# The last layer's MLP: seven half products in three of four chunks, plain ones in the fourth, and low parts on VectorE

## The chip, the cores and the metric

The kernel runs on one core of a Trainium2 chip. The metric is device time in microseconds (us) of one execution. Five engines work side by side, each through its own instructions in order: TensorE (PE; its weight loads are shown as PEld), VectorE (DVE), ScalarE (ACT), GpSimd (POOL) and SyncE (SP), which here issues the DMA transfers. They wait for each other by semaphores. Before the change the median of three runs is 2346.34 us (2345.56 to 2347.01).

## The reference

Two layers of a transformer trunk with a token-mixing half (convolution branch and differential attention) and a channel half. The change touches only the channel half of the second layer, on 512 latent tokens:

```
def sqrelu_mlp(h, w1, w2):
    return jnp.square(jax.nn.relu(h @ w1)) @ w2
...
x = x + gx2 * sqrelu_mlp(modulate(rmsnorm(x, norm2_g[i]), sx2, ax2), w_mlp1[i], w_mlp2[i])
```

h has 1024 columns, w1 is 1024 x 4096 and w2 is 4096 x 1024. All of it is float32, and the result must be as exact as float32.

## The kernel before

**Three matmuls for one.** A float32 operand is split (`split`, lines 75 to 77) into a high part, which ScalarE writes in the format fp32r (L76), and a low part, the rest, which VectorE or GpSimd subtracts (L77). `mm3` then issues three matmuls into the same PSUM bank: high times high (L109), high times low of the moving operand (L110), low of the stationary operand times high (L111).

**Stages.** `last_mixing` takes the 4096 hidden columns in four chunks of 1024. In each chunk the *first products* (`hidden`) compute relu(h w1) squared in four slabs s of 256 columns, 48 matmuls of 512 columns a slab: 192 in a chunk. `operands` turns a slab's result fr into stationary operands. Then the *half products* multiply these with W2's chunk and add to what earlier chunks gave.

**Seven half products.** The chunk's second product is 512 tokens x 1024 by 1024 x 1024. It is cut into quarters: A11, A12, A21, A22 (halves of the tokens by halves of the hidden columns) and B11, B12, B21, B22 of W2. In place of eight products of quarters, seven are made (Winograd's form of Strassen's method): products 1 (A11 B11), 2 (A12 B21), 3 (S4 B22), 4 (A22 T4), 5 (S1 T1), 6 (S2 T2) and 7 (S3 T3), where S1 to S4 are sums of A's quarters (tile sm, L505 to L508) and T1 to T4 sums of B's (`minus`, L578, in place in the tiles r_w). One half product is 2 token tiles x 4 slabs x 3 = 24 matmuls. Products 2, 3 and 4 stay in their PSUM banks through all chunks (`held`); products 1, 5, 6 and 7 go to X, which is free by then (`summed`, L538). In the last chunk the seven are combined, multiplied with the gate row (grow), and x is added; x stands transposed in DRAM (xt_d) and is loaded back.

**Buffers and queues.** High and low parts of weights have two buffers each (tags whi, wlo), which W1's slabs and W2's quarters take in turn: ScalarE can start a new high part only when the last matmul that reads the buffer's former content is done. Raw weights have four buffers of 1 MB (tag raw). sm and aoh, aol (high and low parts of A11 and S1 to S4; A12 and A22 stand in h2hh and h2hl) have one. W2's quarters are split in two halves of 128 x 1024, the first half's low part on VectorE, the second's on GpSimd. The sums' low parts (aol<-sm) are on GpSimd too.

**Order.** A scheduler sets each engine's order when the program is built, from its own estimate of times; on the chip each engine then keeps to it. So an instruction that waits holds everything behind it on its engine.

In the trace, f is a first product, r a half product, h_ and l_ high and low parts (h_w: W1; h_b: a quarter as it is; h_t: a sum T).

## Time and profile before

| | |
|---|---|
| median of three runs | 2346.34 us |
| the profiled execution's own time | 2348.47 us |
| its span, first to last instruction's end | 2346.6 us |
| mean granted TensorE clock in the span | 0.99 |
| TensorE, VectorE, ScalarE, GpSimd busy | 96%, 68%, 44%, 35% |
| moved by DMA | 229.47 MB, mean 98 GB/s |

The span starts at 0; times in the views are us from there. The last layer's MLP begins at about 1974 us. A row of the timeline has the start, the duration, the engine, the line, the operation, the tiles written and read, and in brackets how long the engine had been idle and what ended that. A group row has count, busy us and mean ns of one, and the idle time before. Durations of instructions that follow each other at once overlap a little, so that the distance of their starts, not the duration, is what each costs. In a row of windows stand the stretch, its length, busy us and count of PE, PEld, DVE, ACT and POOL, the granted clock, the DMA engines' busy share and GB/s.

### The profile page before, as it was taken

Reading aid. Unit: us, or ns where it says so; the run is one execution under the profiler, and the core shown is the slowest. Engines: PE = TensorE matmul, PEld = TensorE weight load, DVE = VectorE, ACT = ScalarE, POOL = GpSimd, SP = SyncE. Lnnn points to the kernel's source line nnn. Section 1 sums busy time; section 2 is a strip of 40 time slices with the busy share of each in tenths; the row PEclk is TensorE's granted clock in tenths of the full one; section 3 lists DMA queues with packets and bytes.
Section 4 is the critical chain, followed back from the end, with each engine's and each line's share of the span. In section 5 each row is a group of like instructions: output and inputs, shape, how many; then the busy total and the mean of one; then the engine's idle time right before and its main releaser. Section 6 shows DMA issues by size and latency. Waiting matters only on the chain. (4 is left out here: it accounts for less than half of the span.)

```text
span 2346.6 us, 36460 instructions
## 1 busy us (share of the span) xinstructions
PE 2256.7 (96%) x14530; PEld 2019.1 (86%) x14530; DVE 1586.3 (68%) x2690; ACT 1036.2 (44%) x2007; POOL 813.6 (35%) x843
## 2 busy tenths in 40 slices
PE   8999999999999999999999999999999999999996
PEld 6999998888888998888888998899877779787785
DVE  6777776599666455655546567867769876646658
ACT  5555655522332362332415255656533334554442
POOL 1866764110000142323232266757510001423426
PEclk9999999999999999999999999999999999999999
DMA  9211111134535124333334311210115333233131
GB/s 303 63 36 44 46 46 45 46 128 154 178 125 185 43 80 135 108 126 117 117 117 135 91 62 43 59 44 26 61 54 165 112 115 128 90 126 108 57 128 67
DMA packets 216937, 229.47 MB, mean 98 GB/s; under 512 B 7408, under 2 KB 195776, under 8 KB 216640
## 3 DMA queue, kind: packets, MB, share of 16 engines
q1 hardware_dynamic: 216768, 227.15, 30.4%
q8 instruction: 114, 1.87, 0.3%
q14 instruction: 55, 0.45, 0.1%
HBM read 211.36 MB, written 15.77 MB: 97 GB/s over the span
## 5 line engine op out<-in xcount | busy, mean ns | idle before, releaser
L109 PE MATMUL f<-h2hh,h_w 128*128 128x512 f32 (+1 forms) x832 | 282.1, 342 | 1.7 <-ACT h2hh L76 1.5
L110 PE MATMUL f<-h2hl,h_w 128*128 128x512 f32 (+1 forms) x832 | 282.7, 341 | 1.0 <-POOL h2hl L77 1.0
L111 PE MATMUL f<-h2hh,l_w 128*128 128x512 f32 (+1 forms) x832 | 281.5, 340 | 0.0
L77 POOL TENSOR_TENSOR l_w<-r_w,h_w 128x1024 fp32r<-128x1024 f32 x64 | 157.5, 2482 | 336.5 <-ACT h_w L76 336.5
L1166 DVE SCALAR_TENSOR_TENSOR cacc<-z,cols,cacc 128x783 f32<-128x783 f32 (+1 forms) x240 | 207.9, 918 | 0.3
L109 PE MATMUL qk<-h_wqk,h1h 128*128 128x256 f32 x640 | 183.3, 289 | 2.1 <-ACT rw L758 1.4
L109 PE MATMUL r<-fh,h_w 128*128 128x256 f32 (+1 forms) x576 | 183.7, 319 | 0.3 <-DVE X L1363 0.3
L110 PE MATMUL r<-fl,h_w 128*128 128x256 f32 (+1 forms) x576 | 183.4, 319 | 0.0
L111 PE MATMUL r<-fh,l_w 128*128 128x256 f32 (+1 forms) x576 | 183.2, 318 | 0.0
L110 PE MATMUL qk<-l_wqk,h1h 128*128 128x256 f32 x640 | 180.7, 285 | 0.0
L111 PE MATMUL qk<-h_wqk,h1l 128*128 128x256 f32 x640 | 176.9, 285 | 0.3 <-POOL h1l L77 0.3
L109 PEld LDWEIGHTS f<-h2hh,h_w 128*128 128x128 f32 x832 | 156.6, 189 | 20.3 <-ACT h2hh L76 1.9
L110 PEld LDWEIGHTS f<-h2hl,h_w 128*128 128x128 f32 x832 | 157.5, 190 | 19.3 <-POOL h2hl L77 1.9
L930 DVE TENSOR_REDUCE st<-S 128x1 f32<-128x768 f32 (+1 forms) x160 | 134.4, 845 | 58.5 <-PE S L928 57.3
L111 PEld LDWEIGHTS f<-h2hh,l_w 128*128 128x128 f32 x832 | 157.3, 189 | 17.7
L282 DVE SCALAR_TENSOR_TENSOR adaac<-ar,cvec,adaac 128x256 f32<-128x256 f32 x336 | 152.1, 516 | 20.5 <-ACT adaac L279 15.0
L933 ACT ACTIVATE e<-S,st 128x768 f32<-128x768 f32 (+1 forms) x160 | 130.8, 820 | 39.9 <-DVE st L930 39.7
L76 ACT ACTIVATE h_w<-r_w 128x1024 fp32r<-128x1024 f32 x96 | 96.4, 1052 | 102.5 <-issue 55.2
L109 PE MATMUL gt<-h1h,h_wg 128*128 128x512 f32 (+1 forms) x384 | 138.0, 360 | 0.0
L110 PE MATMUL gt<-h1l,h_wg 128*128 128x512 f32 (+1 forms) x384 | 136.7, 356 | 0.0
L111 PE MATMUL gt<-h1h,l_wg 128*128 128x512 f32 (+1 forms) x384 | 136.6, 356 | 0.0
L109 PEld LDWEIGHTS qk<-h_wqk,h1h 128*128 128x128 f32 x640 | 122.8, 192 | 4.5 <-ACT rw L758 1.6
(316 smaller groups left out, 6795.8 us busy)
## 6 DMA issues: line engine op xcount, KB each, us to landing
r_w<-in_w_mlp_dram SPq DMA_DIRECT2D x64, 1024.0 KB, 5.3
ada<-in_w_ada_dram SPq DMA_DIRECT2D x24, 1024.0 KB, 5.5
ar<-in_w_ada_dram SPq DMA_DIRECT2D x48, 512.0 KB, 3.5
r_wqk<-in_w_in_dram SPq DMA_DIRECT2D x32, 512.0 KB, 5.2
r_wg<-in_w_in_dram SPq DMA_DIRECT2D x16, 1024.0 KB, 5.2
r_wv<-in_w_in_dram SPq DMA_DIRECT2D x8, 1024.0 KB, 5.3
r_wao<-in_w_attn_out_dram SPq DMA_DIRECT2D x8, 1024.0 KB, 5.1
r_wo<-in_w_out_dram SPq DMA_DIRECT2D x8, 1024.0 KB, 5.2
```

Of the source, the lines that this page charges most:

```text
L76: nc.scalar.activation(out=hi, in_=src, func=AF.Copy)
L77: return (lo_eng or nc.vector).tensor_tensor(out=lo, in0=src, in1=f32(hi), op=ALU.subtract)
L109: nc.tensor.matmul(ps, sh, mh, start=first, stop=False)
L110: nc.tensor.matmul(ps, sh, ml, start=False, stop=False)
L111: nc.tensor.matmul(ps, sl, mh, start=False, stop=last)
L282: nc.vector.scalar_tensor_tensor(out=a[:, q], in0=r[:, j], scalar=cvec[:, k, q : q + 1], in1=a[:, q], op0=ALU.mult, op1=ALU.add)
L930: nc.vector.tensor_reduce(out=st[:, m : m + 1], in_=S[:, :nkey], axis=AX.X, op=ALU.max, negate=True)
L933: nc.scalar.activation(out=e[:, :nkey], in_=S[:, :nkey], func=AF.Exp, bias=st[:, m : m + 1], accum_out=st[:, 2 + m : 3 + m])
L1166: nc.vector.scalar_tensor_tensor(out=ca[cc][:, :CV], in0=zt[cc][:, t : t + CV], scalar=wcol, in1=ca[cc][:, :CV], op0=ALU.mult, op1=ALU.add)
```

## The change

In chunks 0 to 2 the seven half products stay. All low parts of W2's quarters and of the sums are now on VectorE, and B11 is loaded and split beside the last slab's first products. In chunk 3, the eight plain products are made: A's quarters are split straight from fr, no sums of A or B are built. The sums of the seven products of chunks 0 to 2 are combined at the head of chunk 3 (`combine`), beside its first products: they are gated, and x is added. The held banks of products 2, 3 and 4 take three quarters' plain products on top of what they hold, C22 gets a bank of its own. Each finished 128 x 512 tile then needs a multiplication with the gate row, an addition and two transfers (`final`). The core of the diff:

```
         def operands(c, s):
...
+            if c == 3:
+                split(AB[0][:, :2, s], AB[1][:, :2, s],
+                      fr[:, 0].rearrange("p (o n) -> p o n", o=2))
+                split(AT[0][:, :, s], AT[1][:, :, s],
+                      fr[:, 1].rearrange("p (o n) -> p o n", o=2))
+                return
...
-            split(AB[0][:, 1:, s], AB[1][:, 1:, s], sm, nc.gpsimd)
+            split(AB[0][:, 1:, s], AB[1][:, 1:, s], sm)
...
-            for k, eng in ((slice(0, 2), nc.vector), (slice(2, 4), nc.gpsimd)):
-                split(hi[:, k], lo[:, k], r[:, k], eng)
+            for k in (slice(0, 2), slice(2, 4)):
+                split(hi[:, k], lo[:, k], r[:, k])
...
+        def combine(step):
+            qs = ((0, 0), (0, 1)) if step == 0 else ((1, 0), (1, 1))
+            xq = fp.tile([P, 2, 2, HN], F32, tag="raw", bufs=4, name=f"xq{step}")
+            nc.sync.dma_start(xq, xt_d[2 * step : 2 * step + 2].rearrange("t h p n -> p t h n"))
+            for t in range(2):
+                m1, m5, m6, m7 = (M[n][:, t] for n in (1, 5, 6, 7))
+                if step == 0:
+                    tt(out=m6, in0=m1, in1=m6, op=ALU.add)
+                    tt(out=m7, in0=m6, in1=m7, op=ALU.add)
+                    tt(out=m6, in0=m6, in1=m5, op=ALU.add)
+                    tt(out=m5, in0=m7, in1=m5, op=ALU.add)
+                for (tq, nq), m in zip(qs, (m1, m6) if step == 0 else (m7, m5)):
+                    tt(out=m, in0=m, in1=gn[nq], op=ALU.mult)
+                    tt(out=m, in0=m, in1=xq[:, t, nq], op=ALU.add)
...
                         for m in range(2):
                             hidden(c, s, m, g)
+                            if (s, m) == (3, 0):
+                                b11 = quarter(c, 0, 0)
+                                w11 = halves_of(b11, f"b11_{c}")
...
+                if c == 3 and ss[0] < 2:
+                    combine(ss[0])
...
+        def final(tq, nq, t):
+            row = (2 * tq + t) * P
+            for j, o in enumerate((slice(0, 256), slice(256, 512))):
+                u = state["xp"].tile([P, 512], F32, tag="u", bufs=3,
+                                     name=f"u{tq}{nq}{t}_{j}")[:, :256]
+                tt(out=u, in0=banks[tq, nq][t][:, o], in1=gn[nq][:, o], op=ALU.mult)
+                tt(out=u, in0=u, in1=parts[tq, nq][:, t, o], op=ALU.add)
+                nc.sync.dma_start(
+                    out[0, row : row + P, HN * nq + o.start : HN * nq + o.stop], u)
+
+        for nq in range(2):
+            for kh in range(2):
+                w = w11 if (kh, nq) == (0, 0) else halves_of(quarter(3, kh, nq), f"b{kh}{nq}_3")
+                for tq in range(2):
+                    a = ((A11, A12), (A21, A22))[tq][kh]
+                    for t in range(2):
+                        product(banks[tq, nq][t], a, w, t, (tq, nq, kh) == (1, 1, 0), kh == 1)
+                        if kh:
+                            final(tq, nq, t)
```

Removed are the last chunk's seven products with the combining that stood between and behind them (before: L600 to L644). Every instruction ahead of the last layer's MLP stands where it did. Three places in the new order follow. In them the first number behind a tile's name is the chunk or the product, the last one only a running number.

VectorE in chunk 1, from the last rows of the first products' operands on (r_w2_1_00 and r_w2_1_11 are the raw tiles of B11 and B22, r1_1_0 is product 1's first tile). Before:

```order
L77 TENSOR_TENSOR aol_20749<-fr1_3_21683,aoh_20748 128x256
L578 TENSOR_TENSOR r_w2_1_01_21751<-r_w2_1_11_21753,r_w2_1_01_21751 128x1024
L506 TENSOR_TENSOR sm1_3_21738<-fr1_3_21683 128x256
L77 TENSOR_TENSOR l_b22_1_21794<-r_w2_1_11_21753,h_b22_1_21793 128x1024
L578 TENSOR_TENSOR r_w2_1_11_21753<-r_w2_1_11_21753,r_w2_1_00_21749 128x1024
L538 TENSOR_TENSOR X2_20130<-X2_20130,r1_1_0_21763 128x512
L505 TENSOR_TENSOR sm1_3_21738<-fr1_3_21683 128x256
```

Now:

```order
L514 TENSOR_TENSOR sm1_2_21664<-fr1_2_21609,sm1_2_21664 128x256
L77 TENSOR_TENSOR aol_20749<-sm1_2_21664,aoh_20748 128x4x256
L77 TENSOR_TENSOR l_b22_1_21794<-r_w2_1_11_21759,h_b22_1_21793 128x1024
L512 TENSOR_TENSOR sm1_3_21746<-fr1_3_21683 128x256
L77 TENSOR_TENSOR l_b22_1_21794<-r_w2_1_11_21759,h_b22_1_21793 128x1024
L543 TENSOR_TENSOR X2_20130<-X2_20130,r1_1_0_21763 128x512
L597 TENSOR_TENSOR r_w2_1_11_21759<-r_w2_1_11_21759,r_w2_1_00_21711 128x1024
L511 TENSOR_TENSOR sm1_3_21746<-fr1_3_21683 128x256
L77 TENSOR_TENSOR h2hl1_20141<-fr1_3_21683,h2hh1_20140 128x2x256
L597 TENSOR_TENSOR r_w2_1_11_21759<-r_w2_1_11_21759,r_w2_1_00_21711 128x1024
L543 TENSOR_TENSOR X2_20130<-X2_20130,r1_1_1_21777 128x512
L513 TENSOR_TENSOR sm1_3_21746<-sm1_3_21746,fr1_3_21683 128x256
```

The low part of sm2 and both halves of B22's low part are now VectorE's, and they stand ahead of the sum T2 (L597, before L578). Behind the last row come T1's low part (two halves), sm3's last row (L514) and sm3's low part.

TensorE in chunk 1, where the held product 3 ends and product 2 (B21) begins. Before:

```order
L109 MATMUL r1_5_1_21845<-h_t1_1_21825,aoh_20748 128x512
L111 MATMUL r_3_0_21255<-h_b22_1_21793,aol_20749 128x512
L111 MATMUL r_3_1_21268<-h_b22_1_21793,aol_20749 128x512
L110 MATMUL r1_5_0_21831<-l_t1_1_21826,aoh_20748 128x512
L111 MATMUL r1_5_0_21831<-h_t1_1_21825,aol_20749 128x512
L109 MATMUL r1_5_0_21831<-h_t1_1_21825,aoh_20748 128x512
```

Now:

```order
L111 MATMUL r_3_0_21255<-h_b22_1_21793,aol_20749 128x512
L111 MATMUL r_3_1_21268<-h_b22_1_21793,aol_20749 128x512
L111 MATMUL r1_5_0_21831<-h_t1_1_21825,aol_20749 128x512
L111 MATMUL r1_5_1_21845<-h_t1_1_21825,aol_20749 128x512
L109 MATMUL r_2_0_21325<-h_b21_1_21861,h2hh1_20140 128x512
L109 MATMUL r_2_1_21338<-h_b21_1_21861,h2hh1_20140 128x512
L110 MATMUL r_2_0_21325<-l_b21_1_21862,h2hh1_20140 128x512
```

Before, twelve matmuls of product 5 stood between product 3's last L111 and product 2's first L109. Now nearly all of product 5 is ahead of them, and two stand between.

VectorE at the end of the program (r_4 are product 4's banks, r3_1 the new bank of C22's second tile; u are the output tiles). Before:

```order
L605 TENSOR_TENSOR X2_20130<-X2_20130,grow_20750 128x512
L635 TENSOR_TENSOR X2_20130<-X2_20130,r_2_1_21338 128x512
L643 TENSOR_TENSOR u0_0_23100<-u0_0_23100,X2_20130 128x256
L643 TENSOR_TENSOR u0_1_23104<-u0_1_23104,X2_20130 128x256
L606 TENSOR_TENSOR X2_20130<-X2_20130,x2_22985 128x512
L605 TENSOR_TENSOR X2_20130<-X2_20130,grow_20750 128x512
L643 TENSOR_TENSOR u1_0_23120<-u1_0_23120,X2_20130 128x256
L606 TENSOR_TENSOR X2_20130<-X2_20130,x11_22877 128x512
L642 TENSOR_TENSOR u1_1_23124<-r_4_1_21406,grow_20750 128x256
L643 TENSOR_TENSOR u1_1_23124<-u1_1_23124,X2_20130 128x256
```

Now:

```order
L628 TENSOR_TENSOR u110_0_23087<-r3_0_22833,grow_20750 128x256
L628 TENSOR_TENSOR u110_1_23091<-r3_0_22833,grow_20750 128x256
L629 TENSOR_TENSOR u110_0_23087<-u110_0_23087,X2_20130 128x256
L629 TENSOR_TENSOR u110_1_23091<-u110_1_23091,X2_20130 128x256
L628 TENSOR_TENSOR u111_0_23107<-r3_1_22834,grow_20750 128x256
L628 TENSOR_TENSOR u111_1_23111<-r3_1_22834,grow_20750 128x256
L629 TENSOR_TENSOR u111_0_23107<-u111_0_23107,X2_20130 128x256
L629 TENSOR_TENSOR u111_1_23111<-u111_1_23111,X2_20130 128x256
```

The rows of 512 columns that combined products have moved ahead, into chunk 3's first products. Behind the last half product's tile stand only its four rows of 256 columns.

## The prediction

> **What bounds the kernel now.** I read the page first, then the stages of the last layer's MLP in the view of windows, then the timeline around the places where TensorE stands still.

> ```profile
> span 2346.6 us, 36460 instructions
> PE 2256.7 (96%) x14530; PEld 2019.1 (86%) x14530; DVE 1586.3 (68%) x2690; ACT 1036.2 (44%) x2007; POOL 813.6 (35%) x843
> ...
> core 0: us, PE busy (x) PEld busy (x) DVE busy (x) ACT busy (x) POOL busy (x), PEclk, DMA share, GB/s
> 2026.04:2069.06 43.02, 40.12 (x169) 32.29 (x168) 21.64 (x18) 20.46 (x25) 20.53 (x8) 0.96 0.33 100
> 2069.06:2112.58 43.52, 43.52 (x193) 36.04 (x192) 24.02 (x30) 23.35 (x34) 7.42 (x4) 1.00 0.29 96
> 2112.58:2155.94 43.36, 39.29 (x170) 31.17 (x168) 29.27 (x25) 16.85 (x18) 21.35 (x8) 1.00 0.33 99
> 2199.46:2243.23 43.77, 40.33 (x169) 32.38 (x168) 27.51 (x25) 16.84 (x18) 20.23 (x8) 0.96 0.31 97
> 2243.23:2286.75 43.52, 43.52 (x193) 36.05 (x193) 24.71 (x31) 22.87 (x33) 7.42 (x4) 1.00 0.29 97
> 2286.75:2332.22 45.47, 39.77 (x169) 30.91 (x167) 38.13 (x35) 14.84 (x16) 32.73 (x14) 1.00 0.18 58
> 2332.22:2346.60 14.38, 0.00 (x1) 0.00 (x0) 11.54 (x18) 0.00 (x0) 7.40 (x5) 0.61 0.31 109
> ```

> TensorE bounds the whole span (96%), so only its idle time, its matmul count and the end after its last matmul can pay. The 43.52 us rows are first products (192 matmuls, one more straddles): no idle, 43.52/192 = 0.2267 us a matmul. The rows of 43.02, 43.36 and 43.77 us are the seven half products of chunks 0, 1 and 2: 168 x 0.2267 = 38.1 us of matmul, so 4.9, 5.3 and 5.7 us lost. Chunk 3 takes 45.47 us for the same 38.1 (7.4 lost), and then come 14.38 us without TensorE. In all 37.7 us here are not matmul. Why they are lost, in chunk 1:

> ```profile
> 2112.13 0.39 PE L110 MATMUL f<-h2hl,h_w 128*128 128x512 f32 x1
> ...
> 2112.40 2.57 POOL L77 TENSOR_TENSOR aol<-sm,aoh 128x1024 fp32r<-128x1024 f32 x1 [6.14 <-ACT aoh L76]
> 2112.56 2.01 ACT L76 ACTIVATE h_b<-r_w 128x1024 fp32r<-128x1024 f32 x2 [0.23 <-PE f L110]
> ...
> 2114.92 2.37 POOL L77 TENSOR_TENSOR l_b<-r_w,h_b 128x1024 fp32r<-128x1024 f32 x1
> 2115.00 2.57 DVE L506 TENSOR_TENSOR sm<-fr 128x256 f32<-128x256 f32 x1 [2.31 <-POOL aol L77]
> ...
> 2115.30 0.61 PE L109 MATMUL r<-h_b,aoh 128*128 128x512 f32 x2
> ...
> 2117.50 1.21 DVE L77 TENSOR_TENSOR l_b<-r_w,h_b 128x1024 fp32r<-128x1024 f32 x1
> ...
> 2118.77 0.50 PE L110 MATMUL r<-l_b,aoh 128*128 128x512 f32 x1 [2.85 <-DVE l_b L77]
> ...
> 2126.17 0.61 PE L109 MATMUL r<-h_t,aoh 128*128 128x512 f32 x2
> 2127.07 0.73 PE L111 MATMUL r<-h_b,aol 128*128 128x512 f32 x2 [0.29 <-POOL aol L77]
> 2128.16 0.50 PE L110 MATMUL r<-l_t,aoh 128*128 128x512 f32 x1 [0.35 <-DVE l_t L77]
> ```

> TensorE waits 2.85 us for the low part of B22 from VectorE. VectorE could have made it at 2113.6, when ACT's first h_b was done, but stood behind L506, which waits for GpSimd's aol (one sm buffer), and then L506 itself took 2.57 us while GpSimd ran l_b. At 2127 and 2128 the next low parts are late in the same way. So the root is GpSimd: its own slow low parts, and VectorE slowed beside it:

> ```profile
> 2102.77 1.23 DVE L77 TENSOR_TENSOR l_b<-r_w,h_b 128x1024 fp32r<-128x1024 f32 x1 [2.61 <-ACT h_b L76]
> 2104.03 3.32 DVE L578 TENSOR_TENSOR r_w<-r_w,r_w 128x1024 f32<-128x1024 f32 x1
> ...
> 2107.61 1.21 DVE L578 TENSOR_TENSOR r_w<-r_w,r_w 128x1024 f32<-128x1024 f32 x1
> 2108.74 0.68 DVE L77 TENSOR_TENSOR h2hl<-fr,h2hh 128x512 fp32r<-128x512 f32 x1
> 2109.35 0.41 DVE L507 TENSOR_TENSOR sm<-sm,fr 128x256 f32<-128x256 f32 x1
> 2109.68 1.21 DVE L578 TENSOR_TENSOR r_w<-r_w,r_w 128x1024 f32<-128x1024 f32 x1
> ...
> L578 DVE TENSOR_TENSOR r_w<-r_w,r_w 128x1024 f32<-128x1024 f32 x32 | 55.1, 1723 | 0.4
> ...
> L77 POOL TENSOR_TENSOR aol<-sm,aoh 128x1024 fp32r<-128x1024 f32 x16 | 39.1, 2442 | 163.5 <-ACT aoh L76 156.2 <-PE r L111 7.3
> ```

> The same L578 takes 1.21 us alone and 3.32 us when a GpSimd low part runs; its mean is 1.72. Read by starts, VectorE alone needs 1.13 us for a 1024-wide row, 0.61 for 512, 0.33 for 256.

> **Chunks 0 to 2, worked out.** Seven second halves and four sums' low parts a chunk go from GpSimd (2.44 us or more each) to VectorE: 11 x 1.13 = 12.4 us. VectorE is busy 24.0 + 29.3 of chunk 1's 86.9 us, and loses the slow-downs, so it has room; only order matters. [...] I call the end of the first products 0 and walk chunk 1 in the changed order.

> VectorE before that: B11's low part starts at 2102.77, which is -9.8. From there eleven instructions (six of 1.13, one of 0.61, four of 0.33) end near -1.0 with sm2. ACT makes its high part (1.06), VectorE its low one: to 1.3. ACT's B22 halves follow at 1.2 and 2.2. Then VectorE: B22 low first half to 2.5, sm3 row, second half to 4.0, the sum of product 1 (0.61), a B row, two short ones, a B row: 7.9, product 1's other sum 8.5, sm row 8.8, T1's low first half about 10.0, its second 11.1, sm3's last row 11.5, ACT 12.6, low part 13.8.

> TensorE: product 1's first tile to 2.7, two L109 of product 3 (high part there at 1.2), the second tile to 5.9, product 3 to 9.5 with low parts there at 2.5 and 4.0: **the 2.85 us wait is gone**. Two L109 of product 5 to 10.0, then L110 needs T1's low part at 10.0 to 10.1: 0.15 us at most. Product 3's last L111 is the 70th matmul: 69 x 0.2267 + 0.15 = 15.8; sm3's low part is there at 13.8.

> A **new wait** comes at B21. Its high tile takes B22's buffer (two buffers), so ACT can start only after product 3's last L111. Above, ACT follows the last reader's start by 2112.56 - 2112.13 = 0.43 us, and takes 1.0: 15.8 + 1.45 = 17.3. TensorE's order has only two matmuls of product 5 between, and is there at 72 x 0.2267 + 0.15 = 16.5: waits 0.8. Two L109 later it needs the low part (17.3 + 1.25 = 18.5; TensorE at 17.75): another 0.8. Before, 12 matmuls of product 5 stood ahead of that L109 and 10 more ahead of the low part, and hid both. After it nothing waits: T3's low part comes at 22, needed at 24. A restart costs about 0.1 once. So 38.1 + 0.15 + 0.8 + 0.8 + 0.1 = 40.0 us; chunk 2 has the same order; in chunk 0 ACT copies the sums, and T1 comes earlier (39.9). Three times 40.0 against 130.15 us: **-10.1**. No wait over 1 us is left, so I also count no time at a lower clock: the clock column has 0.96 only in stages with such a wait (chunks 0 and 2; chunks 1 and 3 have it and 1.00). Bounds: 0 us of waits (-15.9), and all as now (0).

> **Chunk 3.** One half product more: 24 x 0.2267 = +5.4. Against it all 7.4 us of its stalls, if nothing new waits. The operands are plain splits without sm. B11 is split while the last first products run; 42 matmuls of it remain (9.5 us) and cover the next quarter (ACT 2.0 + VectorE 1.1 after the buffer is released, 3.6 us). Each later quarter has 48 matmuls (10.9 us) of cover. So 192 x 0.2267 = 43.5 against 45.47: **-2.0**. The 24 combining rows (24 x 0.61 = 14.6 us) move into the first products' stretch, where VectorE is idle 43.52 - 24.71 = 18.8 us, and loses the sm rows there. Their two x transfers go ahead of W1's second and third slab on SP, each about

> ```profile
> r_w<-in_w_mlp_dram SPq DMA_DIRECT2D x64, 1024.0 KB, 5.3
> ```

> long; the slab behind xq0's buffer starts when the combining lets it go, about 19 us in, and is needed at 8 x 24 x 0.2267 x 3/4 = 32.6: 24.3 plus 2 for the halves fits by 6 us. I take 0; bounds 0 and 3.

> **The end.**

> ```profile
> 2331.83 0.40 PE L111 MATMUL r<-h_t,h2hl 128*128 128x512 f32 x1
> ...
> 2333.43 0.68 DVE L605 TENSOR_TENSOR X<-X,grow 128x512 f32<-128x512 f32 x1
> ...
> 2337.37 1.07 DVE L642 TENSOR_TENSOR u<-r,grow 128x256 f32<-128x256 f32 x3
> ...
> 2343.37 0.42 DVE L643 TENSOR_TENSOR u<-u,X 128x256 f32<-128x256 f32 x1
> 2343.82 0.33 SPq L644 DMA_DIRECT2D out_dram<-u  x1
> ...
> out_dram<-u SPq DMA_DIRECT2D x4, 128.0 KB, 1.7
> ```

> VectorE works off combining for 11.5 us after the last matmul. Changed, only four 256-wide rows follow it: 0.1 + 3 x 0.33 + 0.42 = 1.5, issue at once, 1.7 to landing, and 1.1 from that landing (2345.5) to the span's end: 4.3, with 0.2 for the matmul end and a u buffer (three, a 1.7 us transfer each): 4.5. **-9.9**; bounds 3.9 and 7.5 (if the last row waits a whole transfer).

> Sum -10.1 - 2.0 - 9.9 = **-22.0**: span 2324.6. The profiled execution took 2348.47 us by its own clock, 2.1 over the median of 2346.34, so I take the difference from the median: **2324.3 us**.

> **Rivals.** (1) *The move buys nothing in chunks 0 to 2*: VectorE's queue takes over what GpSimd did, and TensorE waits 5.3 us a chunk as now. For: the new wait at B21, and a one-engine queue. Against: L506's wait and the 3.32 us rows vanish with GpSimd. 2334.4 us, 0.10.
> (2) *No wait is left in them*: if the buffers are released sooner or VectorE runs ahead, 3 x 1.9 = 5.7 less: 2318.6, 0.10.
> (3) *Slower: VectorE becomes the bound*. If L578's 1.72 us mean is its own and not GpSimd's doing, VectorE stays that slow and the added halves and low parts ahead of B21 (B22, T1, B21, sm2, sm3) stand on the path: 5 x 1.72 = 8.6 us more wait a chunk, 25.8 - 11.9 = +13.9: 2360 us. It turns slower from 11.9/3 = 4.0 us a chunk. Against: two rows of 1.21 us in the same stage with GpSimd idle. 0.03.
> (4) *The last chunk starves*: xq or a W1 slab late, or the final rows held by three u buffers; 5 to 10 us: about 2332, 0.10.
> The rest, 0.67, is my forecast with its own range of 2320 to 2329.

> **Numbers.** No change within 0.2% means 2341.6 to 2351.0; it needs (1) and (4) together and more: 0.04. Slower 0.03, faster 0.93. The range that takes in the bounds of the waits and most of (1) and (4): 2318 to 2333.

> **What would show it.** Right: the product stages of chunks 0 to 2 near 40 us with a wait of about 0.8 us at h_b and one at l_b of B21, none of 2.85; clock 1.00 in them; no GpSimd row after norm 2; L597 at 1.2 us; 192 gapless matmuls in chunk 3; 4 to 5 us from the last matmul to the end. Wrong: a wait at l_t of product 5 over 1 us (VectorE late), a gap before a first product of chunk 3 (x or W1 late), L597 near 1.7, a tail over 7.

## The result, and the profile after

The changed kernel takes **2327.78 us** (median of six runs, 2325.58 to 2331.33), and the kernel before 2347.19 us in the runs beside it: ratio **0.9917, interval 0.9904 to 0.9929**, that is 19.4 us less. Predicted were 2324.3 us, with 2318 to 2333 as the range. The profiled execution took 2328.47 us with a span of 2326.7 us, 19.9 less than before's 2346.6.

The page of the changed kernel begins:

```profile
span 2326.7 us, 36416 instructions
...
PE 2256.1 (97%) x14554; PEld 2021.1 (87%) x14554; DVE 1572.8 (68%) x2720; ACT 1026.7 (44%) x1997; POOL 682.5 (29%) x789
```

The same view of windows as in the prediction, cut at the start of each stage's first matmul. Rows: product stage of chunk 0, first products of chunk 1, product stage of chunk 1, product stage of chunk 2, chunk 3's first products (with six early matmuls of B11 among them), the rest of chunk 3's products, the end.

```profile
core 0: us, PE busy (x) PEld busy (x) DVE busy (x) ACT busy (x) POOL busy (x), PEclk, DMA share, GB/s
2026.08:2065.94 39.86, 38.64 (x170) 31.38 (x169) 25.28 (x25) 20.39 (x26) 0.00 (x0) 1.00 0.35 109
2065.94:2109.46 43.52, 43.52 (x194) 36.04 (x193) 24.14 (x33) 23.20 (x33) 0.00 (x0) 1.00 0.29 94
2109.46:2149.74 40.28, 38.73 (x170) 31.30 (x169) 29.65 (x32) 16.78 (x19) 0.00 (x0) 1.00 0.35 107
2193.26:2235.19 41.93, 40.37 (x170) 32.46 (x168) 30.32 (x33) 16.77 (x19) 0.00 (x0) 0.96 0.32 103
2235.19:2280.07 44.88, 44.88 (x200) 37.16 (x198) 28.41 (x40) 20.77 (x30) 0.00 (x0) 1.00 0.41 138
2280.07:2322.40 42.33, 42.32 (x187) 34.72 (x185) 17.84 (x35) 7.75 (x9) 0.00 (x0) 1.00 0.13 43
2322.40:2326.70 4.30, 0.00 (x0) 0.00 (x0) 1.42 (x4) 0.00 (x0) 0.00 (x0) 0.88 0.22 73
```

GpSimd has no row left in any of them. Where the time went, by stage:

| Stage | before | changed | difference | predicted |
|---|---|---|---|---|
| products of chunk 0 | 43.02 | 39.86 | -3.16 | -3.0 |
| products of chunk 1 | 43.36 | 40.28 | -3.08 | -3.4 |
| products of chunk 2 | 43.77 | 41.93 | **-1.84** | -3.8 |
| chunk 3, first products and products | 43.52 + 45.47 | 44.88 + 42.33 | -1.78 | -2.0 |
| the end | 14.38 | 4.30 | -10.08 | -9.9 |
| sum | | | -19.9 | -22.0 |

The products began at 2026.04 us before and at 2026.08 after, so nothing came from ahead of them. One row is off: chunk 2, and its clock column says 0.96 where chunks 0 and 1 say 1.00.

What TensorE waited for between 2026 and 2322 us, in the view of waits (total, times, longest):

```profile
PE r L110 <- DVE l_b L77: 2.2, 3, 0.9
PE r L109 <- ACT h_b L76: 2.1, 3, 0.7
```

Once a chunk each: these are the two waits at B21. The 2.85 us wait for B22's low part is gone, and nothing else of this size is left. The timeline of chunk 2 at that place:

```profile
2209.20 0.61 PE L111 MATMUL r<-h_t,aol 128*128 128x512 f32 x2
2209.40 2.01 ACT L76 ACTIVATE h_b<-r_w 128x1024 fp32r<-128x1024 f32 x2 [3.71 <-PE r L111]
2209.63 1.29 DVE L543 TENSOR_TENSOR X<-X,r 128x512 f32<-128x512 f32 x2 [2.68 <-PE r L111]
2210.51 0.73 PE L109 MATMUL r<-h_b,h2hh 128*128 128x512 f32 x2 [0.69 <-ACT h_b L76]
2210.83 2.35 DVE L77 TENSOR_TENSOR l_b<-r_w,h_b 128x1024 fp32r<-128x1024 f32 x2
...
2212.11 0.50 PE L110 MATMUL r<-l_b,h2hh 128*128 128x512 f32 x1 [0.86 <-DVE l_b L77]
...
2213.24 0.63 PE L111 MATMUL r<-h_b,h2hl 128*128 128x512 f32 x1
2213.66 0.63 PE L109 MATMUL r<-h_b,h2hh 128*128 128x512 f32 x1
2214.09 0.63 PE L110 MATMUL r<-l_b,h2hh 128*128 128x512 f32 x1
```

ACT can begin B21's high part only when product 3's last L111 has let go of the buffer (2209.40), and TensorE has two matmuls of product 5 to do meanwhile. By starts of matmuls (0.23 us apart where nothing waits) it loses 0.85 us there. VectorE then still has two L543 rows, the sums of product 5, ahead of the low part: 1.03 us more. After 2213 the matmuls stand 0.42 us apart in place of 0.23, though nothing is late any more: TensorE runs at half its clock (0.50 in the clock column from 2213.01 to 2216.43 us, quoted below). In chunk 1 the same two waits (0.85 and 1.03 us) were followed by matmuls 0.23 us apart.

VectorE alone, two groups between 1973 and 2327 us:

```profile
L597 DVE TENSOR_TENSOR r_w<-r_w,r_w 128x1024 f32<-128x1024 f32 x24 | 29.1, 1218 | 0.0
L512 DVE TENSOR_TENSOR sm<-fr 128x256 f32<-128x256 f32 x12 | 5.1, 422 | 6.5 <-ACT fr L497 6.1
```

The sum over W2 (before: L578 with a mean of 1723 ns) takes 1218 ns, L512 422 (before: L506 with 955), and neither waits for GpSimd. The end:

```profile
2322.00 0.39 PE L111 MATMUL r<-h_b,h2hl 128*128 128x512 f32 x1
2322.43 0.76 DVE L628 TENSOR_TENSOR u<-r,grow 128x256 f32<-128x256 f32 x2 [1.30 <-PE r L111]
2323.10 0.75 DVE L629 TENSOR_TENSOR u<-u,X 128x256 f32<-128x256 f32 x2
2323.54 0.81 SPq L630 DMA_DIRECT2D out_dram<-u  x2
```

Four short rows follow the last matmul, as the order says.

### The profile page after: what moved, and what is told of

It is laid out like the page before. It is cut to its first block, busy times and chain, and to the rows that moved or that the text cites. A ratio compares the mean times of both kernels' runs of the same rounds, so it can differ in the third digit from the quotient of the medians.

```text
span 2326.7 us, 36416 instructions
## 1 busy us (share of the span) xinstructions
PE 2256.1 (97%) x14554; PEld 2021.1 (87%) x14554; DVE 1572.8 (68%) x2720; ACT 1026.7 (44%) x1997; POOL 682.5 (29%) x789
## 4 chain that ended last, share of the span: by engine, by line
PE 78%; DVE 11%; POOL 4%; ACT 3%; DMA 2%; issue 1%; SPq 0%; DVEq 0%; POOLq 0%; ACTq 0%
PE f L109 6%; PE f L110 6%; PE f L111 6%; PE r L110 6%; PE r L111 6%; PE r L109 6%; DVE cacc L1163 3%; PE qk L109 2%; PE qk L110 2%; PE qk L111 2%; PE gt L109 2%; PE gt L110 2%; PE gt L111 2%; PE o L109 2%; PE o L110 2%; PE o L111 2%
## 5 line engine op out<-in xcount | busy, mean ns | idle before, releaser
L109 PE MATMUL f<-h2hh,h_w 128*128 128x512 f32 (+1 forms) x832 | 282.1, 342 | 1.7 <-ACT h2hh L76 1.5
L110 PE MATMUL f<-h2hl,h_w 128*128 128x512 f32 (+1 forms) x832 | 282.7, 341 | 1.0 <-POOL h2hl L77 1.0
L111 PE MATMUL f<-h2hh,l_w 128*128 128x512 f32 (+1 forms) x832 | 281.5, 340 | 0.0
L77 POOL TENSOR_TENSOR l_w<-r_w,h_w 128x1024 fp32r<-128x1024 f32 x64 | 157.2, 2479 | 336.7 <-ACT h_w L76 336.7
L109 PE MATMUL qk<-h_wqk,h1h 128*128 128x256 f32 x640 | 182.9, 288 | 2.1 <-ACT rw L755 1.4
L109 PE MATMUL r<-fh,h_w 128*128 128x256 f32 (+1 forms) x576 | 183.7, 319 | 0.2 <-DVE X L1360 0.2
L110 PE MATMUL r<-fl,h_w 128*128 128x256 f32 (+1 forms) x576 | 183.4, 319 | 0.0
L111 PE MATMUL r<-fh,l_w 128*128 128x256 f32 (+1 forms) x576 | 183.2, 318 | 0.0
L110 PE MATMUL qk<-l_wqk,h1h 128*128 128x256 f32 x640 | 180.4, 284 | 0.1
L111 PE MATMUL qk<-h_wqk,h1l 128*128 128x256 f32 x640 | 176.5, 284 | 0.3 <-POOL h1l L77 0.3
L109 PEld LDWEIGHTS f<-h2hh,h_w 128*128 128x128 f32 x832 | 156.6, 189 | 20.3 <-ACT h2hh L76 1.9
L110 PEld LDWEIGHTS f<-h2hl,h_w 128*128 128x128 f32 x832 | 157.5, 190 | 19.3 <-POOL h2hl L77 1.9
L111 PEld LDWEIGHTS f<-h2hh,l_w 128*128 128x128 f32 x832 | 157.3, 189 | 17.6
L76 ACT ACTIVATE h_w<-r_w 128x1024 fp32r<-128x1024 f32 x96 | 96.4, 1052 | 102.6 <-issue 45.0
L109 PE MATMUL gt<-h1h,h_wg 128*128 128x512 f32 (+1 forms) x384 | 138.1, 360 | 0.0
L110 PE MATMUL gt<-h1l,h_wg 128*128 128x512 f32 (+1 forms) x384 | 136.7, 356 | 0.0
L111 PE MATMUL gt<-h1h,l_wg 128*128 128x512 f32 (+1 forms) x384 | 136.5, 356 | 0.0
L109 PEld LDWEIGHTS qk<-h_wqk,h1h 128*128 128x128 f32 x640 | 122.4, 191 | 4.4 <-ACT rw L755 1.6
## 6 DMA issues: line engine op xcount, KB each, us to landing
r_w<-in_w_mlp_dram SPq DMA_DIRECT2D x64, 1024.0 KB, 5.4
ada<-in_w_ada_dram SPq DMA_DIRECT2D x24, 1024.0 KB, 5.5
r_wg<-in_w_in_dram SPq DMA_DIRECT2D x16, 1024.0 KB, 5.1
r_wv<-in_w_in_dram SPq DMA_DIRECT2D x8, 1024.0 KB, 5.1
r_wao<-in_w_attn_out_dram SPq DMA_DIRECT2D x8, 1024.0 KB, 5.4
r_wo<-in_w_out_dram SPq DMA_DIRECT2D x8, 1024.0 KB, 5.2
```

The lines of the kernel that those rows point to most:

```text
L76: nc.scalar.activation(out=hi, in_=src, func=AF.Copy)
L77: return (lo_eng or nc.vector).tensor_tensor(out=lo, in0=src, in1=f32(hi), op=ALU.subtract)
L109: nc.tensor.matmul(ps, sh, mh, start=first, stop=False)
L110: nc.tensor.matmul(ps, sh, ml, start=False, stop=False)
L111: nc.tensor.matmul(ps, sl, mh, start=False, stop=last)
```

## The experiments

All are built from the changed kernel, or, in the first, from the one before. Stage times are those of the view of windows, as above. Beside the times stand those of the kernel before and of the changed kernel on the same chip, where they were run with it.

### Which part of the change pays in chunks 0 to 2

**The move alone**, in the kernel before (combining behind the products, seven half products in all four chunks, B11 split where it was):

```diff
-            split(AB[0][:, 1:, s], AB[1][:, 1:, s], sm, nc.gpsimd)
+            split(AB[0][:, 1:, s], AB[1][:, 1:, s], sm)
...
-            for k, eng in ((slice(0, 2), nc.vector), (slice(2, 4), nc.gpsimd)):
-                split(hi[:, k], lo[:, k], r[:, k], eng)
+            for k in (slice(0, 2), slice(2, 4)):
+                split(hi[:, k], lo[:, k], r[:, k])
```

> The kernel before, with only the low parts (second halves of W2, sums) moved from GpSimd to VectorE; seven products in all four chunks, B11 split where it was, combining at the end. Theory (GpSimd's slow rows and the rows they slow are the root of the waits in chunks 0 to 2): the 2.85 us wait goes in every chunk, the B21 wait of 1 to 2 us may come, so 2.5 to 3 us a chunk less in four chunks, 9 to 12 us in all: about 2337 us (2335 to 2339). [...] Rival B (VectorE becomes the bound, L578's 1.72 us is its own): over 2352 us, L578 still at 1.7 us with GpSimd idle.

Measured: 2336.28 us (2335.80 to 2338.99) against 2347.32, ratio 0.9957 [0.9943, 0.9971], 11.0 us less. Its windows, the product stages of the four chunks and the end:

```profile
2024.53:2064.42 39.89, 38.67 (x169) 31.38 (x168) 25.27 (x25) 20.40 (x26) 0.00 (x0) 1.00 0.35 108
2107.94:2148.23 40.29, 38.74 (x170) 31.30 (x168) 29.65 (x32) 16.78 (x19) 0.00 (x0) 1.00 0.35 108
2191.75:2233.65 41.90, 40.35 (x170) 32.46 (x168) 29.65 (x32) 16.77 (x19) 0.00 (x0) 0.96 0.33 103
2277.17:2319.53 42.36, 40.72 (x169) 32.33 (x167) 37.41 (x41) 14.76 (x17) 9.66 (x6) 0.96 0.19 62
2319.53:2334.50 14.97, 0.01 (x1) 0.00 (x0) 12.12 (x19) 0.00 (x0) 7.91 (x5) 0.64 0.30 105
```

The first three stages are those of the changed kernel to 0.03 us. So the move by itself makes all of their gain (130.15 - 122.08 = 8.1 us), and 3.1 us in chunk 3, whose seven products it finds there. The end stays at 15 us. "The move" is here the other engine together with the order that the scheduler makes of it, and in the traces TensorE's order changes as well. Product 1's second tile now stands ahead of product 3's first L110, so that B22's low part is needed by the 27th matmul of the stage and not by the 15th, and the twelve matmuls of product 5 ahead of B21 become two.

**Everything but the move**:

```diff
-            split(AB[0][:, 1:, s], AB[1][:, 1:, s], sm)
+            split(AB[0][:, 1:, s], AB[1][:, 1:, s], sm, nc.gpsimd)
...
-            for k in (slice(0, 2), slice(2, 4)):
-                split(hi[:, k], lo[:, k], r[:, k])
+            second = nc.vector if "_3" == name[-2:] else nc.gpsimd
+            for k, eng in ((slice(0, 2), nc.vector), (slice(2, 4), second)):
+                split(hi[:, k], lo[:, k], r[:, k], eng)
```

> The changed kernel, with the low parts of chunks 0 to 2 back on GpSimd; plain last chunk, combining and early B11 as changed. Theory: the three product stages lose what the move gave, 130.15 - 122.1 = 8.1 us, so 2335.9 us (2334 to 2338); last chunk and end as changed (43.5 and 4.3 us). Rival A (early B11 carries the chunks, the move nothing): 2327 to 2329 us. Rival B (last chunk and end carry less than their 12 us): over 2339 us.

Measured: 2337.73 us (2334.66 to 2338.40) against 2347.32 before, ratio 0.9957 [0.9944, 0.9969]. Its product stages:

```profile
2025.21:2068.30 43.09, 40.19 (x170) 32.34 (x169) 21.65 (x18) 20.46 (x25) 20.53 (x8) 0.96 0.32 100
2111.82:2155.16 43.34, 39.30 (x169) 31.16 (x168) 29.27 (x25) 16.84 (x18) 21.33 (x8) 1.00 0.33 100
2198.68:2242.40 43.72, 40.30 (x169) 32.38 (x168) 27.70 (x26) 16.85 (x18) 20.18 (x8) 0.96 0.30 99
```

43.09, 43.34 and 43.72 us, where the kernel before had 43.02, 43.36 and 43.77: 130.15 us in both. TensorE has the order of the kernel before in these stages. Its chunk 3 and the end take 87.20 and 4.30 us, as in the changed kernel (44.88 + 42.33 and 4.30): these two gains need nothing of the move. Had the move bought nothing in chunks 0 to 2 (the prediction's rival 1), these stages would take as long as the changed kernel's 122.07 us; the 8.1 us between them are against that.

**B11 late again**, with all the rest of the change: its quarter is loaded and split behind the operands of the last slab.

```diff
-                            if (s, m) == (3, 0):
-                                b11 = quarter(c, 0, 0)
-                                w11 = halves_of(b11, f"b11_{c}")
...
+            b11 = quarter(c, 0, 0)
+            w11 = halves_of(b11, f"b11_{c}")
             if c == 3:
                 break
```

> The changed kernel, with B11's quarter loaded and split behind the operands of the last slab again, in all chunks. Theory (early B11 only takes two rows out of the way before the products): chunks 0 to 2 lose at most 1 us each, chunk 3, where nothing stands ahead of its first product, 1 to 3 us: 2328 to 2333 us. Rival A (early B11 is what removed the 2.85 us waits): 8 us or more lost in chunks 0 to 2, over 2335 us.

Measured: 2323.77 us (2323.06 to 2329.28) against 2347.32 before, ratio 0.9906 [0.9892, 0.9919], an interval that overlaps the changed kernel's. Its profiled execution, at 2329.28 us the longest of its four, has stages of 39.89, 40.28 and 41.92 us and no wait in chunk 3 either. So the early split buys nothing: the later place was early enough, in chunk 3 too, where I had expected 1 to 3 us. From the first product to the end of the span it takes 2327.5 - 2026.86 = 300.6 us, and the changed kernel 2326.7 - 2026.08 = 300.6 too. The lower median is not from here: the products begin at 2022.8 to 2029.0 us in the profiles of these kernels, whose code ahead of them is the same, and the times spread by as much.

**Half of the move each**: with only the sums' low parts back on GpSimd,

```diff
-            split(AB[0][:, 1:, s], AB[1][:, 1:, s], sm)
+            split(AB[0][:, 1:, s], AB[1][:, 1:, s], sm, nc.gpsimd)
```

> The changed kernel with only the low parts of the sums back on GpSimd; W2's halves all on VectorE. Theory A (the one sm buffer is the root: VectorE's next sum waits for GpSimd's slow sum, and rows beside it take 3.3 us): most of the 8.1 us comes back, 1.5 to 2.7 us a chunk, 2332 to 2336 us. Theory B (W2's second halves on GpSimd are the root): 2327 to 2330 us, stages near 40 to 41 us.

and with only the second halves of W2 there in chunks 0 to 2:

```diff
-            for k in (slice(0, 2), slice(2, 4)):
-                split(hi[:, k], lo[:, k], r[:, k])
+            second = nc.vector if "_3" == name[-2:] else nc.gpsimd
+            for k, eng in ((slice(0, 2), nc.vector), (slice(2, 4), second)):
+                split(hi[:, k], lo[:, k], r[:, k], eng)
```

> The changed kernel with only the second halves of W2's low parts back on GpSimd in chunks 0 to 2; the sums' low parts on VectorE. Theory A (the sm buffer is the root): 2326 to 2330 us, since VectorE's queue is shorter by seven rows a chunk and no sum waits. Theory B (W2's second halves are the root, slow themselves and slowing VectorE): 2331 to 2336 us.

Measured beside the changed kernel's 2326.80 us on the same chip: 2332.05 us (2330.18 to 2337.35) with the sums on GpSimd, 2329.25 us (2327.77 to 2332.31) with W2's halves there. The ratios to before are 0.9937 [0.9923, 0.9951] and 0.9924 [0.9911, 0.9937], against 0.9912 [0.9898, 0.9926]. The times alone put only the sums apart from the changed kernel, whose longest run took 2329.55 us; with W2's halves the times overlap. In the profiles the three product stages sum to 128.42 and 123.64 us, against 122.09 in the changed kernel's profile beside them, +6.3 and +1.6. The 1.6 is a net figure. With W2's halves on GpSimd the stages take 41.08, 41.28 and 41.28 us, all with 1.00 in the clock column, while the changed kernel's chunk 2 has the half clock (41.92 us, where chunk 1 takes 40.29). Without that the waits cost 3.2 us more, so the two halves don't simply add up to the 8.1 of the move. VectorE's rows, first with the sums on GpSimd:

```profile
L77 DVE TENSOR_TENSOR l_b<-r_w,h_b 128x1024 fp32r<-128x1024 f32 x26 | 34.8, 1377 | 30.1 <-ACT h_b L76 30.0
L597 DVE TENSOR_TENSOR r_w<-r_w,r_w 128x1024 f32<-128x1024 f32 x24 | 29.1, 1217 | 0.0
L512 DVE TENSOR_TENSOR sm<-fr 128x256 f32<-128x256 f32 x11 | 4.6, 416 | 9.5 <-ACT fr L497 6.2 <-POOL aol L77 3.3
```

then with W2's halves there (its L598 is L597 in the others):

```profile
L598 DVE TENSOR_TENSOR r_w<-r_w,r_w 128x1024 f32<-128x1024 f32 x24 | 47.7, 1996 | 0.3
L77 DVE TENSOR_TENSOR l_b<-r_w,h_b 128x1024 fp32r<-128x1024 f32 x17 | 25.7, 1530 | 25.1 <-ACT h_b L76 25.1
```

The kernel in which VectorE is slowed most (1996 ns for the sum over W2, 1530 for the low parts) loses less than the other. That is not because its slowed rows are free. In chunk 1 there:

```profile
2110.37 2.97 POOL L77 TENSOR_TENSOR l_b<-r_w,h_b 128x1024 fp32r<-128x1024 f32 x1 [8.45 <-ACT h_b L76]
...
2111.12 3.31 DVE L598 TENSOR_TENSOR r_w<-r_w,r_w 128x1024 f32<-128x1024 f32 x1
...
2117.47 0.42 DVE L514 TENSOR_TENSOR sm<-fr,sm 128x256 f32<-128x256 f32 x1
...
2119.03 0.50 PE L109 MATMUL r<-h_b,aoh 128*128 128x512 f32 x1 [1.10 <-ACT aoh L76]
```

Beside GpSimd's row the sum takes 3.31 us in place of 1.22. VectorE is then busy without a pause up to sm3's last row (L514), so sm3's high part comes late, and TensorE waits 1.10 us for it. The 2.1 us that the sum lost are more than this wait. What this kernel is spared are the two waits at B21: at that place TensorE has the order of the kernel before again, with thirteen matmuls of product 5 between product 3's last L111 and B21's first L109. It also comes to B22's low part at its 15th matmul, as in the kernel before, and does not wait there. So the 2.85 us wait hung mainly on the sums' low parts, and it goes without a new order of TensorE.

With the sums on GpSimd VectorE is hardly slower by the mean, but at one place it counts. In chunk 1 there:

```profile
2113.17 2.41 POOL L77 TENSOR_TENSOR aol<-sm,aoh 128x1024 fp32r<-128x1024 f32 x1 [13.23 <-ACT aoh L76]
...
2114.07 3.72 DVE L77 TENSOR_TENSOR l_b<-r_w,h_b 128x1024 fp32r<-128x1024 f32 x2 [2.13 <-ACT h_b L76]
...
2116.72 0.50 PE L110 MATMUL r<-l_b,aoh 128*128 128x512 f32 x1 [0.47 <-DVE l_b L77]
```

GpSimd's sum runs just when VectorE makes B22's low part: the two halves take 3.72 us, where two such halves took 2.35 in the changed kernel, and TensorE waits. Here too TensorE needs B22's low part by its 15th matmul, and the two waits at B21 are those of the changed kernel. So the sums are the larger root, but not in the way that theory A put it: the wait for the one sm buffer is 3.3 us in all of the last MLP, and the delay of B22's low part and of what follows it is what TensorE sees. In neither of these kernels does TensorE keep the changed kernel's order, and none was run that holds the order fixed, so how each figure divides between the slower engine and the order stays open.

### What is left at B21, and the clock

**Product 2 ahead of product 3.** If the two waits come from the buffer that product 3's last L111 holds, then they go where B21 is split before B22, into a buffer that has long been free. T2, which needs B22 unsplit, moves behind:

```diff
-            b12, b22, b21 = (quarter(c, *q) for q in ((0, 1), (1, 1), (1, 0)))
+            b12, b21, b22 = (quarter(c, *q) for q in ((0, 1), (1, 0), (1, 1)))
...
-            w22 = halves_of(b22, f"b22_{c}")
+            w21 = halves_of(b21, f"b21_{c}")
             for t in range(2):
-                held(3, c, S4, w22, t)
+                held(2, c, A12, w21, t)
             minus(b12, b22, b12)
             summed(5, c, S1, halves_of(b11, f"t1_{c}"))
-            minus(b22, b22, b11)
-            w21 = halves_of(b21, f"b21_{c}")
+            w22 = halves_of(b22, f"b22_{c}")
             for t in range(2):
-                held(2, c, A12, w21, t)
+                held(3, c, S4, w22, t)
+            minus(b22, b22, b11)
             minus(b21, b21, b22)
```

> The changed kernel, in chunks 0 to 2 with B21's product 2 ahead of B22's product 3. B21's high part then takes a buffer that is free early, and B22's takes the one that product 2 lets go, which does not wait for sm3. Theory (the waits at B21 come from the buffer that product 3's last L111 holds, and with them the half clock in chunk 2): both waits and the half clock go, stages of 38.3 to 39 us in place of 39.9, 40.3 and 41.9: 5 to 6 us less than the changed kernel, about 2322 us (2321 to 2324). Rival (VectorE's queue is late in any order, the wait only moves to B22's or T1's low part): 2326 to 2330 us with a wait of 1 us or more at l_b or l_t.

Measured: 2319.36 us (2317.59 to 2321.58) against 2347.32 before, ratio **0.9882 [0.9869, 0.9896]**. Once more on another chip, with the changed kernel beside it:

> The version with product 2 (B21) ahead of product 3 (B22), once more, beside the changed kernel on one chip. Three product stages of 38.1 us without a wait, no half clock between 2020 us and the last matmul: 7 to 9 us less than the changed kernel, 2317 to 2321 us. If the first 2319 us came from that chip and not from the order: within 2 us of the changed kernel.

> The changed kernel beside it: 2325 to 2330 us, stages of 39.9, 40.3 and 41.9 us (40.3 in chunk 2 where the two waits fall into two stretches of the clock's grid).

Measured: 2321.22 us (2318.24 to 2323.63), ratio to before 0.9888 [0.9875, 0.9901]; the changed kernel there 2329.45 us (2324.79 to 2335.62), 0.9921 [0.9907, 0.9936]. So this order is 8.2 us below the changed kernel, and the two intervals don't meet. From the first product to the end the profiles take 292.9 us, and the changed kernel 300.6. Its product stages in the first profile:

```profile
2022.97:2061.05 38.08, 38.08 (x169) 31.53 (x168) 25.46 (x25) 20.40 (x26) 0.00 (x0) 1.00 0.37 113
2104.57:2142.66 38.09, 38.09 (x170) 31.48 (x169) 29.74 (x32) 16.79 (x19) 0.00 (x0) 1.00 0.37 114
2186.18:2224.26 38.08, 38.08 (x169) 31.48 (x168) 29.96 (x33) 16.78 (x19) 0.00 (x0) 1.00 0.34 113
```

TensorE is busy in all of each stage: 168 matmuls of 0.2267 us. That is 7.8 us less than 122.07, more than I had expected (5 to 6): I had left up to 0.9 us a stage for waits elsewhere, and there are none. VectorE is as busy as in the changed kernel, 85.16 us against 85.25: its load never was the limit.

**Why the clock halves in chunk 2 and not in chunk 1.** The trace records when the granted clock changes. In the twelve profiled executions there are 112 stretches at 0.50, and within each execution all of them begin at whole multiples of 3.413 us from one another, to 5 ns; all but the last of each execution, which reaches into its end, are one or two such steps long. Counting the matmul records by the steps of this grid (from 100 us on, and where the clock was full in the step itself):

| Matmul time in a step of 3.413 us | steps | next step at half clock |
|---|---|---|
| under 1.45 us | 72 | 72 |
| 1.45 to 1.9 us | 45 | 23 |
| over 1.9 us | 7601 | 1 |

So in these records TensorE need not stand still for a whole step: half clock followed each of the 72 steps with less than 1.45 us of matmul. This also tells apart the chunks of the kernel before, which all had the wait for B22's low part: the step with that wait held 1.10 us of matmul in chunk 0 and 0.57 in chunk 2 (from 2028.27 and 2202.35 us), and half clock followed; it held 1.66 in chunk 1 (from 2117.02), and full clock followed. Between 1.45 and 1.9 us this count alone doesn't decide, and what else counts there stays open. The steps of the grid around B21 in the changed kernel, two in chunk 1 and two in chunk 2:

```profile
2124.27:2127.68 3.41, 2.49 (x10) 1.42 (x8) 1.84 (x3) 2.07 (x3) 0.00 (x0) 1.00 0.22 77
2127.68:2131.09 3.41, 2.78 (x12) 2.34 (x13) 3.41 (x4) 1.83 (x2) 0.00 (x0) 1.00 0.00 0
2209.60:2213.01 3.41, 1.85 (x7) 1.07 (x7) 3.38 (x4) 3.41 (x4) 0.00 (x0) 1.00 0.03 10
2213.01:2216.43 3.42, 3.42 (x10) 2.67 (x9) 3.42 (x4) 0.29 (x1) 0.00 (x0) 0.50 0.00 0
```

In chunk 1 the two waits fall into two steps (2.49 and 2.78 us of matmul), in chunk 2 both into one (1.85 us), and the next is at half clock, with 10 matmuls in its row, where 17 stand in one at full clock (the last row quoted below). The 1.85 us lie in the band of the table in which both happen, at its upper end. In chunk 0 both waits fall into one step too (from 2042.35 us), but the second is shorter (0.69 us): 2.19 us of matmul are left, and the clock stays full. If this is the cause, a shift of chunk 2 against the grid takes it away. The shift is seven matmuls more at the head of chunk 2's first products, whose sum the real ones overwrite:

```diff
             ps = mm_tile(f"f{i}_{c}_{s}_{m}_{g.start}")
+            if (c, s, m) == (2, 0, 0):
+                for k in range(7):
+                    nc.tensor.matmul(ps[:, :W], w[0][:, k, :P], h2hl[0][:, k, g],
+                                     start=k == 0, stop=k == 6)
             fm_block(ps[:, :W], w, m * P, lambda k: (h2hl[0][:, k], h2hl[1][:, k]), g)
```

> The changed kernel with seven matmuls of 512 columns more in chunk 2's first products (1.59 us of TensorE; their sum is overwritten), so that chunk 2's product stage stands 1.6 us later against the grid on which the clock's half stretches begin (all of them lie whole multiples of 3.413 us apart within one run). Waits at B21 are the same 0.85 and 1.03 us. Theory (the clock halves after a stretch of the grid in which TensorE had less than about half of its time in matmuls; in chunk 2 both waits fall into one such stretch, in chunk 1 they fall into two): with the shift the waits part, no half clock in chunk 2, its stage 40.3 us in place of 41.9, and the kernel's time that of the changed one (+1.6 - 1.65), 2325 to 2330 us. Rival (waits of this length halve the clock at this place whatever the phase): half clock again, stage 41.9, 1.6 us slower than the changed kernel.

Beside it ran the changed kernel:

> The changed kernel once more, beside these on one chip: 2325 to 2331 us. By the theory of the grid its waits at B21 are the same in every profile (0.85, then 0.7 in chunk 0 and 1.03 in chunks 1 and 2), and only the phase decides where the clock halves.

Measured: 2327.89 us (2325.21 to 2331.24) with the shift, 2326.80 us (2325.86 to 2329.55) without, ratios 0.9916 [0.9903, 0.9930] and 0.9912 [0.9898, 0.9926]: 1.1 us apart, which these spreads can't tell from nothing nor from the rival's 1.6. The profiles can: from the first product to the end of the span they take 2323.4 - 2022.81 = 300.6 us with the seven matmuls more, and 2324.1 - 2023.44 = 300.7 without. The product stages of the shifted kernel:

```profile
2022.81:2062.70 39.89, 38.67 (x170) 31.39 (x168) 25.28 (x25) 20.40 (x26) 0.00 (x0) 1.00 0.35 108
2106.22:2146.51 40.29, 38.74 (x169) 31.30 (x168) 29.65 (x32) 16.78 (x19) 0.00 (x0) 1.00 0.35 107
2191.62:2231.93 40.31, 38.76 (x169) 31.31 (x168) 30.31 (x33) 16.78 (x19) 0.00 (x0) 1.00 0.34 107
```

In this one profile chunk 2 takes 40.31 us, as chunk 1 does, at full clock. The waits are still 0.85 and 1.03 us; by the steps of this execution's grid they now lie in two:

```profile
2206.19:2209.60 3.41, 2.71 (x11) 1.61 (x9) 1.59 (x3) 1.82 (x2) 0.00 (x0) 1.00 0.28 94
2209.60:2213.01 3.41, 2.55 (x12) 2.11 (x12) 3.41 (x4) 2.08 (x3) 0.00 (x0) 1.00 0.00 0
2213.01:2216.43 3.42, 3.42 (x17) 2.84 (x16) 3.09 (x3) 0.12 (x1) 0.00 (x0) 1.00 0.00 0
```

The changed kernel beside it, on the same chip, had 41.92 us in chunk 2 with 0.96 in the clock column, as in all three of its profiles. In every profile with these two waits and no shift (the changed kernel three times, the move alone, B11 late, the sums on GpSimd) both fell into one step in chunk 2, with 1.85 to 1.86 us of matmul, and half clock followed in all six. What holds the phase so steady from execution to execution was not looked into and stays open.

## Why the prediction was right, and where it was off

- **The root in chunks 0 to 2** was named rightly: GpSimd's low parts and the VectorE rows beside them. The move alone makes the gain, and everything but the move leaves the stages at 130.15 us. That the 2.85 us wait goes without a new order of TensorE is shown by the kernel with W2's halves on GpSimd; what share of the rest is the order's is not shown.
- **The walk through chunk 1** holds row by row. From the end of the first products B22's low halves were done at 2.4 and 3.9 us (predicted 2.5 and 4.0), T1's first at 9.8 (10.0), and ACT began B21's high part at 16.2 (16.23). The new wait at B21 is where it was put and has its size at h_b: 0.85 us for 0.8. The 2.85 us wait is gone.
- **The step that failed** is the sentence "No wait over 1 us is left, so I also count no time at a lower clock". In the twelve profiles the half clock went with the sum of matmul time in one step of a grid of 3.413 us, not with the length of the longest wait: chunk 2's two waits in one step were followed by it in all six profiles that have them there, and in the one that parts them it did not come. Chunk 2 measured 41.93 us for 40.0. Of these 1.9 us the half clock is 41.93 - 40.28 = 1.65, the difference to chunk 1, which has the same waits. The prediction had seen that the 2.85 us wait brought 0.96 in chunks 0 and 2 and 1.00 in chunk 1, and took the length as the cause all the same. The 4.9 and 5.7 us that it called lost in chunks 0 and 2 therefore hold a step at half clock each.
- **A mis-sized term** beside it: the wait at l_b, 0.8 predicted, 1.03 measured in chunks 1 and 2. The two L543 sums of product 5 stand ahead of B21's low part on VectorE, and the walk left them out. In chunk 0, where ACT does these sums, it was 0.69. And by starts TensorE lost another 0.11 us behind each of the two waits, where the prediction counted 0.1 once. With the clock this makes -8.1 for -10.1.
- **Chunk 3** came out as -1.8 for -2.0: no gap in its 192 matmuls, x and W1 in time, the combining beside the first products. The early B11, to which I gave the cover of the first quarter, is not needed for it.
- **The end** is 4.30 us for 4.5: -10.1 for -9.9. The upper bound of 7.5 us was loose: one transfer of 1.7 us on top of 4.5 makes 6.2.
- **The rivals.** That the move buys nothing (1) fell with the kernel that leaves it out. That no wait is left (2) did not happen, but the other order of products 2 and 3 shows what it is worth: 7.8 us in the stages, where I had put 5.7; 1.65 of the 7.8 are the half clock, which the 5.7 left out. That VectorE becomes the bound (3) fell: L597 takes 1.22 us, and a stage with as much VectorE work runs without any wait. The last chunk did not starve (4).

## What to carry to other kernels

Before moving work to a faster engine (here 1.22 us for a low part of 128x1024 on VectorE, 2.44 to 2.73 on GpSimd by the means of its groups), walk the rows in their new order, and look at which rows the waiting engine needs next: the mean of a slowed row didn't tell its cost here (1996 ns for the sum over W2 went with a net loss of 1.6 us, 1217 ns with one of 6.3), which depended on whether its result, or that of a row behind it, was needed next. When an edit lets the scheduler make a new order, compare the order too, for a difference between two kernels can come from there. When a walk finds a new wait at a buffer, ask at once whether an exchange of two independent products gives the buffer time to come free; here that was worth 7.8 us more in these stages, nearly as much as the move itself. And look in the trace at how TensorE's idle time lies in the steps of 3.413 us that the clock's records here begin on, not only at each wait: here waits of 0.85 and 1.03 us in one step were followed by a step at half clock, 1.65 us that no wait in the trace shows.
